# Rotary embedding on one core: tables loaded to 64 partitions and spread by a matmul, x's first piece issued by ScalarE, first group in pieces of 2, 2 and 4 rows

## The chip, the core and the metric

The kernel runs on one core of one Trainium2 chip. The metric is the device time of one execution in microseconds; the figure given for a kernel is the median of several runs. Engines are named as in the profile: PE (TensorE; PEld is its weight load), DVE (VectorE), ACT (ScalarE), POOL (GpSimd), SP (SyncE, which here only issues DMAs).

## What is computed

Rotary position embedding on x of 16 batches, 512 positions, 16 heads of 64 elements, in fp32. Each head is cut into halves of 32; cos and sin have one row of 32 per position.

```python
x = x.reshape(batch, seq, num_heads, head_dim)
x1, x2 = x[..., :half_dim], x[..., half_dim:]
rotated = np.concatenate([x1 * cos - x2 * sin, x1 * sin + x2 * cos], axis=-1)
```

x is 33.5 MB, the output as much; cos and sin are 64 KB each.

## The kernel before

The 8192 positions (batch times sequence) are cut into 8 groups of 1024. A group is 128 partitions with 8 successive positions ("rows") each: 2 batches of 64 partitions. A row is 128 x 1024 fp32, a group 4 MB, contiguous 32 KB per partition. The 64 rows are numbered u = 0 to 63, and live in a ring of 40 (RING), which is 5 groups; the result is written over x in place.

A row's result is the sum of two products. The first, t1 = x * cos, is made by DVE into PSUM (mul, L247; three buffers). The second, t2 = (halves of x swapped) * (-sin, sin), is made by POOL into SBUF (L216; six buffers), except for row 3 of each group (VROW), where DVE makes it too (L238). The sum is made in one of two ways: for rows 1, 3 and 6 of each group, PE adds t2 to t1 in PSUM by four matmuls with the identity (L187), and ACT copies the result back to x's place (L161); for the other five, DVE adds (comb, L258). DVE's order is written out: mul(u), then the add of row u - 2. A product t1 of row u needs the buffer of row u - 3, so it waits for that row's add or, where PE added, for ACT's copy.

Loads are issued by SP in order (on_sync, L138): the first group in two halves of 2 MB, the others whole. After the first half come cos and sin (L145), each to all 128 partitions (two batches need the same rows, so each row is read twice), 1 KB per partition. The first five groups' loads wait for nothing; the loads of groups 5, 6 and 7 wait until the store of group 0, 1 and 2 has landed (L141). Stores are issued by ACT between its copies (L165), one for each group, the last group in two halves.

Before the rows start, DVE copies cos into PSUM (L225) and row 3's sin with both signs (L227, L228); ACT writes sin with both signs to s_sb for POOL (L154, L155); POOL builds the identity (L198, L200); PE clears t1's banks with six matmuls of zeros (L173).

Of the kernel before, what the change touches and what calls it, by code (L numbers as in the profile page):

```python
# [6 lines left out]
def bass_split_heads_rope_kernel(  # L7
# [4 lines left out]
    num_heads: bass.AP,  # L12
    out: bass.AP,
):

# [23 lines left out]
    RING = 40  # L39
    NU = G * R  # L40

    def pieces(halved):
        return [
            (g, r, n) for g in range(G) for r, n in (((0, R // 2), (R // 2, R // 2)) if g == halved else ((0, R),))
        ]


    loads = pieces(0)
    stores = pieces(G - 1)
    load_of = [c for c, (_, _, n) in enumerate(loads) for _ in range(n)]  # L50

    def where(u):
# [9 lines left out]
    def count(flags):  # L62
        return [sum(flags[: u + 1]) for u in range(NU)]

    n_pool = count([not v for v in V2])
    n_dve = count(V2)
    n_pe = count(PE2)
    n_comb = count([not a for a in PE2])

# [6 lines left out]
    with ExitStack() as stack:  # L76
        x_sb = stack.enter_context(nc.sbuf_tensor([P, RING, H, 2, HALF], fp32))
        t2_sb = stack.enter_context(nc.sbuf_tensor([P, NT2, H, 2, HALF], fp32))
        stage = stack.enter_context(nc.sbuf_tensor([P, 2, R * HALF], fp32))
        s_sb = stack.enter_context(nc.sbuf_tensor([P, R, 2, HALF], fp32))  # L80
        ident = stack.enter_context(nc.sbuf_tensor([P, P], fp32))
        zero = stack.enter_context(nc.sbuf_tensor([P, BANK], bf16))
        tab_ps = stack.enter_context(nc.psum_tensor([P, BANK], fp32))
        t1_ps = stack.enter_context(nc.psum_tensor([P, NT1, H * HD], fp32))
        sem_in = [stack.enter_context(nc.semaphore(f"in{c}")) for c in range(len(loads))]
        sem_out = [stack.enter_context(nc.semaphore(f"out{c}")) for c in range(G - RING // R)]
# [6 lines left out]
        sem_i = stack.enter_context(nc.semaphore("ident"))  # L93
        sem_w = stack.enter_context(nc.semaphore("bits"))
        sem_p = stack.enter_context(nc.semaphore("pool"))
        sem_d = stack.enter_context(nc.semaphore("dve2"))
        sem_m = stack.enter_context(nc.semaphore("mul"))
        sem_v = stack.enter_context(nc.semaphore("comb"))
        sem_e = stack.enter_context(nc.semaphore("pe"))
        sem_a = stack.enter_context(nc.semaphore("act"))  # L100

        c_ps = tab_ps[:, 0:R * HALF].rearrange("p (r d) -> p r d", d=HALF)
        s_ps = tab_ps[:, R * HALF:R * HALF + HD].rearrange("p (t d) -> p t d", d=HALF)

        xv = x.rearrange("(g b) (s r) d -> g s b (r d)", b=BL, r=R)
        ov = out.rearrange("(g b) (s r) h d -> g s b (r h d)", b=BL, r=R)
# [22 lines left out]
        def wait_t2_free(eng, u):  # L129

            if u >= NT2:
# [3 lines left out]
                else:  # L135
                    eng.wait_ge(sem_v, n_comb[v])

        def on_sync(sp):  # L138
            for c, (g, r, n) in enumerate(loads):
                if g * R >= RING:  # L140
                    sp.wait_ge(sem_out[g - RING // R], 16)  # L141
                sp.dma_start(tile(g, r, n), part(xv, g, r, n)).then_inc(sem_in[c], 16)  # L142
                if c == 0:
                    for i, (table, sem) in enumerate(((cos, sem_cos), (sin, sem_sin))):
                        sp.dma_start(  # L145
                            stage[:, i, :],
                            table.rearrange("(s r) d -> s (r d)", r=R)[:, None, :].broadcast_to([SB, BL, R * HALF]),
                        ).then_inc(sem, 16)
            sp.wait_ge(sem_rest, 16 * (len(stores) - len(sem_out)))

        def on_scalar(ae):
            ae.wait_ge(sem_sin, 16)
            sv = stage[:, 1, :].rearrange("s (r d) -> s r d", d=HALF)
            ae.activation(s_sb[:, :, 0, :], sv, COPY, scale=-1.0)  # L154
            ae.activation(s_sb[:, :, 1, :], sv, COPY).then_inc(sem_s, 1)  # L155
            ends = {g * R + r + n - 1: (c, g, r, n) for c, (g, r, n) in enumerate(stores)}
            for u in range(NU):
                k = where(u)[2]
                if PE2[u]:
                    ae.wait_ge(sem_e, n_pe[u])  # L160
                    ae.activation(xs[:, k, :], t1_ps[:, u % NT1, :], COPY).then_inc(sem_a, 1)  # L161
                if u in ends:
                    c, g, r, n = ends[u]
                    wait_added(ae, u)
                    ae.dma_start(part(ov, g, r, n), tile(g, r, n)).then_inc(  # L165
                        sem_out[c] if c < len(sem_out) else sem_rest, 16
                    )

        def on_tensor(pe):
            pe.wait_ge(sem_z, 1)  # L170
            for k in range(NT1):
                for b in range(EH):
                    pe.matmul(  # L173
                        t1_ps[:, k, b * BANK:(b + 1) * BANK], zero[:, 0:P], zero[:], start=True, stop=True
                    ).then_inc(sem_w, 1)
            pe.wait_ge(sem_i, 2)
            for u in range(NU):
                if not PE2[u]:
                    continue
                pe.wait_ge(sem_m, u + 1)  # L180
                if V2[u]:
                    pe.wait_ge(sem_d, n_dve[u])
                else:
                    pe.wait_ge(sem_p, n_pool[u])
                t2 = t2_sb[:, u % NT2, :, :, :].rearrange("p h t d -> p (h t d)")
                for b in range(EH):
                    ins = pe.matmul(  # L187
                        t1_ps[:, u % NT1, b * BANK:(b + 1) * BANK],
                        ident[:],
                        t2[:, b * BANK:(b + 1) * BANK],  # L190
                        start=False,
                        stop=True,
                        skip_group_check=True,
                    )
                ins.then_inc(sem_e, 1)

        def on_gpsimd(pl):
            pl.memset(ident[:], 1.0).then_inc(sem_i, 1)  # L198
            pl.wait_ge(sem_i, 1)
            pl.affine_select(  # L200
                out=ident[:],
                in_=ident[:],
                compare_op=mybir.AluOpType.is_equal,
                fill=0.0,
                base=0,
                pattern=[[-1, P]],
                channel_multiplier=1,
            ).then_inc(sem_i, 1)
            pl.wait_ge(sem_s, 1)
            for u in range(NU):  # L210
                if V2[u]:
                    continue
                c, r, k = where(u)
                pl.wait_ge(sem_in[c], 16)
                wait_t2_free(pl, u)
                pl.tensor_tensor(  # L216
                    t2_sb[:, u % NT2, :, :, :], swapped(k), over_heads(s_sb[:, r]), mult
                ).then_inc(sem_p, 1)

        def on_vector(ve):  # L220
            ve.memset(zero[:], 0.0).then_inc(sem_z, 1)  # L221
            cv = stage[:, 0, :].rearrange("s (r d) -> s r d", d=HALF)
            sv = stage[:, 1, VROW * HALF:(VROW + 1) * HALF]
            ve.wait_ge(sem_cos, 16)
            ve.tensor_copy(c_ps, cv)  # L225
            ve.wait_ge(sem_sin, 16)
            ve.tensor_scalar_mul(s_ps[:, 0, :], sv, -1.0)  # L227
            ve.tensor_copy(s_ps[:, 1, :], sv).then_inc(sem_c, 1)  # L228
            ve.wait_ge(sem_c, 1)
            ve.wait_ge(sem_w, NT1 * EH)  # L230

            def mul(u):
                c, r, k = where(u)
                if u == 0 or load_of[u] != load_of[u - 1]:
                    ve.wait_ge(sem_in[c], 16)
                if V2[u]:
                    wait_t2_free(ve, u)
                    ve.tensor_tensor(  # L238
                        t2_sb[:, u % NT2, :, :, :], swapped(k), over_heads(s_ps), mult
                    ).then_inc(sem_d, 1)  # L240
# [68 lines left out]
```

## Time and profile before

| what | value |
|---|---|
| median of 7 runs | 162.04 us (162.02 to 162.95) |
| profiled execution: its own time | 162.43 us |
| profiled execution: span of its instructions | 161.0 us |
| DVE / POOL busy | 131.6 / 130.6 us |
| first row product on DVE / on POOL starts | 9.76 / 10.25 us |
| cos / sin issued | 1.46 / 2.11 us |
| first store issued (ACT's queue) | 32.08 us |
| last load issued, and lands | 96.9 and 128.8 us |
| last store issued, and its time to landing | 154.24 and 6.7 us |

The span begins with the first instruction and ends with the last; the execution's own time has 1.43 us around it. In the page, section 2 cuts the span into 40 slices of 4 us and shows each engine's busy share in tenths, the DMA engines' mean share and the GB/s that they moved. Other views give the busy times in chosen stretches, the instructions in order of time, and each DMA's issue with its time to landing. A share of the DMA engines a little above 1 in a stretch comes from packets that overlap or that began before it.

### The profile page before, as it was taken

To read this page: it belongs to the slowest core of one execution; us is meant where nothing else is said; L and a number is where in the kernel's file an instruction comes from. 1 tells how busy PE (TensorE), PEld (TensorE's weight loads), DVE (VectorE), ACT (ScalarE), POOL (GpSimd) and SP (SyncE) were. 2 spreads that over 40 slices of the span, in tenths; PEclk is the share of its full clock that TensorE was granted. 3 is DMA by queue.
4 is the path that set the end of the run, shared out by engine and by line. 5 is a ranking of instruction groups with operands and counts; after the bars stand their busy time and mean duration, and the time that the engine had idled before them with its cause. 6 is when DMAs were issued, how large, how long until landed. Compare 5 with 4: busy or idle time off the path is not lost.

```text
span 161.0 us, 579 instructions
## 1 busy us (share of the span) xinstructions
PE 85.6 (53%) x102; PEld 26.9 (17%) x102; DVE 131.6 (82%) x116; ACT 26.6 (17%) x27; POOL 130.6 (81%) x62
## 2 busy tenths in 40 slices
PE   6002928368438549439448448646426844855800
PEld 1001402112202202202202211211111210220200
DVE  0079199999699969998799989997999969996920
ACT  3010220220220220220220221022202022022020
POOL 1049999999999999999997999799979799892000
PEclk9999985555955555855555855595975595555595
DMA  4999999998999999999999999999999999999987
GB/s 138 400 446 497 407 415 480 407 391 383 407 464 431 399 464 433 399 472 431 391 474 440 391 472 440 391 464 448 391 448 456 399 440 464 399 440 448 387 370 326
DMA packets 2882, 67.39 MB, mean 419 GB/s; under 512 B 320, under 2 KB 576, under 8 KB 576
## 3 DMA queue, kind: packets, MB, share of 16 engines
q1 hardware_dynamic: 1584, 33.82, 49.8%
q10 hardware_dynamic: 1296, 33.56, 48.4%
q14 instruction: 2, 0.02, 0.0%
HBM read 33.82 MB, written 33.55 MB: 418 GB/s over the span
## 4 chain that ended last, share of the span: by engine, by line
DVE 30%; PE 23%; issue 17%; POOL 14%; ACT 6%; DMA 5%; SPq 1%; DVEq 0%; POOLq 0%
PE t_ps L187 23%; DVE x_sb L258 15%; POOL t_sb L216 14%; DVE t_ps L247 11%; ACT x_sb L161 6%; DMA stage<-in_sin_dram 5%; DVE t_sb L238 4%; SPq L142 0%; SPq L145 0%; ACT s_sb L154 0%; ACT s_sb L155 0%; DVEq L246 0%; POOLq L134 0%
## 5 line engine op out<-in xcount | busy, mean ns | idle before, releaser
L216 POOL TENSOR_TENSOR t_sb<-x_sb,s_sb 128x1024 f32<-128x1024 f32 x56 | 129.9, 2357 | 14.5 <-ACT s_sb L155 8.9
L187 PE MATMUL t_ps<-t_sb,ident 128*128 128x512 f32 x96 | 82.8, 1016 | 66.3 <-DVE t_ps L247 52.6
L247 DVE TENSOR_TENSOR t_ps<-x_sb,tab_ps 128x1024 f32<-128x1024 f32 x64 | 77.3, 1227 | 13.7 <-ACT x_sb L161 11.9
L258 DVE TENSOR_TENSOR x_sb<-t_ps,t_sb 128x1024 f32<-128x1024 f32 x40 | 48.6, 1216 | 0.0
L187 PEld LDWEIGHTS t_ps<-t_sb,ident 128*128 128x128 f32 x96 | 26.1, 299 | 122.5 <-DVE t_ps L247 87.5
L161 ACT ACTIVATE x_sb<-t_ps 128x1024 f32<-128x1024 f32 x24 | 24.6, 1024 | 119.5 <-PE t_ps L187 119.5
L238 DVE TENSOR_TENSOR t_sb<-x_sb,tab_ps 128x1024 f32<-128x1024 f32 x8 | 9.7, 1209 | 0.0
L225 DVE COPY tab_ps<-stage 128x256 f32<-128x256 f32 x1 | 0.4, 428 | 7.9 <-DMA stage<-in_cos_dram 7.9
L173 PE MATMUL t_ps<-zero 128*128 128x512 bf16 x6 | 2.7, 630 | 1.3 <-DVE zero L221 1.3
L154 ACT ACTIVATE s_sb<-stage 128x256 f32<-128x256 f32 x1 | 0.4, 416 | 7.4 <-DMA stage<-in_sin_dram 7.4
L154 ACT ACT_TABLE_LOAD x1 | 1.3, 1283 | 0.8 <-PEq L291 0.8
L173 PEld LDWEIGHTS t_ps<-zero 128*128 128x128 bf16 x6 | 0.7, 138 | 2.3 <-DVE zero L221 1.2
L221 DVE MEMSET zero<- 128x256 uint32 x1 | 0.3, 272 | 0.9 <-PEq L291 0.9
L198 POOL MEMSET ident<- 128x128 f32 x1 | 0.2, 205 | 0.3 <-POOLq L291 0.3
L155 ACT ACTIVATE s_sb<-stage 128x256 f32<-128x256 f32 x1 | 0.4, 400 | 0.0
L200 POOL TENSOR_SCALAR_AFFINE_SELECT ident<-ident 128x128 f32<-128x128 f32 x1 | 0.3, 293 | 0.1
L291 POOL MEMSET const-float32-0.0<- 128x1 f32 x1 | 0.1, 99 | 0.3 <-issue 0.3
L227 DVE TENSOR_SCALAR tab_ps<-stage 128x32 f32<-128x32 f32 x1 | 0.2, 195 | 0.0
L228 DVE COPY tab_ps<-stage 128x32 f32<-128x32 f32 x1 | 0.2, 184 | 0.0
L291 POOL MEMSET const-uint8-127<- 128x1 uint8 x1 | 0.1, 103 | 0.0
L291 POOL MEMSET const-bfloat16-1.0<- 128x1 bf16 x1 | 0.1, 102 | 0.0
L291 POOL MEMSET const-float32-1.0<- 128x1 f32 x1 | 0.1, 100 | 0.0
## 6 DMA issues: line engine op xcount, KB each, us to landing
x_sb<-in_x_dram SPq DMA_DIRECT2D x7, 4096.0 KB, 31.9
out_dram<-x_sb ACTq DMA_DIRECT2D x7, 4096.0 KB, 27.6
x_sb<-in_x_dram SPq DMA_DIRECT2D x2, 2048.0 KB, 9.8
out_dram<-x_sb ACTq DMA_DIRECT2D x2, 2048.0 KB, 7.3
stage<-in_cos_dram SPq DMA_DIRECT2D x1, 128.0 KB, 7.6
stage<-in_sin_dram SPq DMA_DIRECT2D x1, 128.0 KB, 7.3
```

Source lines behind the costliest of these rows:

```text
L154: ae.activation(s_sb[:, :, 0, :], sv, COPY, scale=-1.0)
L155: ae.activation(s_sb[:, :, 1, :], sv, COPY).then_inc(sem_s, 1)
L161: ae.activation(xs[:, k, :], t1_ps[:, u % NT1, :], COPY).then_inc(sem_a, 1)
L173: pe.matmul(t1_ps[:, k, b * BANK:(b + 1) * BANK], zero[:, 0:P], zero[:], start=True, stop=True).then_inc(sem_w, 1)
L187: ins = pe.matmul(t1_ps[:, u % NT1, b * BANK:(b + 1) * BANK], ident[:], t2[:, b * BANK:(b + 1) * BANK], start=False, stop=True, skip_group ...
L200: pl.affine_select(out=ident[:], in_=ident[:], compare_op=mybir.AluOpType.is_equal, fill=0.0, base=0, pattern=[[-1, P]], channel_multiplier=1,
L216: pl.tensor_tensor(t2_sb[:, u % NT2, :, :, :], swapped(k), over_heads(s_sb[:, r]), mult).then_inc(sem_p, 1)
L225: ve.tensor_copy(c_ps, cv)
L238: ve.tensor_tensor(t2_sb[:, u % NT2, :, :, :], swapped(k), over_heads(s_ps), mult).then_inc(sem_d, 1)
L247: ve.tensor_tensor(t1_ps[:, u % NT1, :].rearrange("p (h d) -> p h d", d=HALF), x_sb[:, k, :, :, :].rearrange("p h t d -> p (h t) d"), c_ps ...
L258: ve.tensor_tensor(xs[:, k, :], t1_ps[:, u % NT1, :], t2_sb[:, u % NT2, :, :, :].rearrange("p h t d -> p (h t d)"), add,).then_inc(sem_v, 1)
L291: nc = _bacc.Bacc("TRN2", target_bir_lowering=False, num_devices=1)
```

## The change

The tables are loaded once, to 64 partitions (stage and the new pick have 64), and one matmul with a 64 x 128 selection matrix puts partition s's rows on partitions 2s and 2s + 1, into one PSUM bank that holds cos and sin. DVE reads cos straight from there; ACT makes s_sb from there; row 3's signed sin has a bank of its own (v_ps) and is written by DVE after ACT is done. The selection matrix is built by POOL ahead of the identity. SP issues the tables first and then the loads from the second piece on; the first piece is issued by ACT as its first instruction. The first group's load is in pieces of 2, 2 and 4 rows. PE no longer waits for DVE's second product of row 3 by a semaphore of its own; DVE's later mul of the same row stands for it.

```diff
-    loads = pieces(0)
-    stores = pieces(G - 1)
+    loads = pieces(0, (2, 2, 4))
+    stores = pieces(G - 1, (4, 4))
...
-        stage = stack.enter_context(nc.sbuf_tensor([P, 2, R * HALF], fp32))
+        stage = stack.enter_context(nc.sbuf_tensor([SB, 2, R * HALF], fp32))
+        pick = stack.enter_context(nc.sbuf_tensor([SB, SB, BL], fp32))
...
-        tab_ps = stack.enter_context(nc.psum_tensor([P, BANK], fp32))
+        tab_ps = stack.enter_context(nc.psum_tensor([P, 2, R, HALF], fp32))
+        v_ps = stack.enter_context(nc.psum_tensor([P, BANK], fp32))
...
-        c_ps = tab_ps[:, 0:R * HALF].rearrange("p (r d) -> p r d", d=HALF)
-        s_ps = tab_ps[:, R * HALF:R * HALF + HD].rearrange("p (t d) -> p t d", d=HALF)
+        c_ps = tab_ps[:, 0]
+        s_ps = v_ps[:, 0:HD].rearrange("p (t d) -> p t d", d=HALF)
...
+        def load(eng, c):
+            g, r, n = loads[c]
+            if g * R >= RING:
+                eng.wait_ge(sem_out[g - RING // R], 16)
+            eng.dma_start(tile(g, r, n), part(xv, g, r, n)).then_inc(sem_in[c], 16)
+
         def on_sync(sp):
-            for c, (g, r, n) in enumerate(loads):
-                if g * R >= RING:
-                    sp.wait_ge(sem_out[g - RING // R], 16)
-                sp.dma_start(tile(g, r, n), part(xv, g, r, n)).then_inc(sem_in[c], 16)
-                if c == 0:
-                    for i, (table, sem) in enumerate(((cos, sem_cos), (sin, sem_sin))):
-                        sp.dma_start(
-                            stage[:, i, :],
-                            table.rearrange("(s r) d -> s (r d)", r=R)[:, None, :].broadcast_to([SB, BL, R * HALF]),
-                        ).then_inc(sem, 16)
+            for i, (table, sem) in enumerate(((cos, sem_cos), (sin, sem_sin))):
+                sp.dma_start(stage[:, i, :], table.rearrange("(s r) d -> s (r d)", r=R)).then_inc(sem, 16)
+            for c in range(1, len(loads)):
+                load(sp, c)
...
         def on_scalar(ae):
-            ae.wait_ge(sem_sin, 16)
-            sv = stage[:, 1, :].rearrange("s (r d) -> s r d", d=HALF)
-            ae.activation(s_sb[:, :, 0, :], sv, COPY, scale=-1.0)
-            ae.activation(s_sb[:, :, 1, :], sv, COPY).then_inc(sem_s, 1)
+            load(ae, 0)
+            ae.wait_ge(sem_t, 1)
+            ae.activation(s_sb[:, :, 0, :], tab_ps[:, 1], COPY, scale=-1.0)
+            ae.activation(s_sb[:, :, 1, :], tab_ps[:, 1], COPY).then_inc(sem_s, 1)
...
+            pe.wait_ge(sem_g, 2)
+            pe.wait_ge(sem_cos, 16)
+            pe.wait_ge(sem_sin, 16)
+            pe.matmul(
+                tab_ps[:].rearrange("p c r d -> p (c r d)"),
+                pick[:].rearrange("q s b -> q (s b)"),
+                stage[:].rearrange("q c f -> q (c f)"),
+                start=True,
+                stop=True,
+            ).then_inc(sem_t, 1)
             pe.wait_ge(sem_i, 2)
...
                 pe.wait_ge(sem_m, u + 1)
-                if V2[u]:
-                    pe.wait_ge(sem_d, n_dve[u])
-                else:
+
+                if not V2[u]:
                     pe.wait_ge(sem_p, n_pool[u])
...
         def on_gpsimd(pl):
+
+            pl.memset(pick[:], 1.0).then_inc(sem_g, 1)
+            pl.wait_ge(sem_g, 1)
+            pl.affine_select(
+                out=pick[:],
+                in_=pick[:],
+                compare_op=mybir.AluOpType.is_equal,
+                fill=0.0,
+                base=0,
+                pattern=[[-1, SB], [0, BL]],
+                channel_multiplier=1,
+            ).then_inc(sem_g, 1)
...
             ve.memset(zero[:], 0.0).then_inc(sem_z, 1)
-            cv = stage[:, 0, :].rearrange("s (r d) -> s r d", d=HALF)
-            sv = stage[:, 1, VROW * HALF:(VROW + 1) * HALF]
-            ve.wait_ge(sem_cos, 16)
-            ve.tensor_copy(c_ps, cv)
-            ve.wait_ge(sem_sin, 16)
-            ve.tensor_scalar_mul(s_ps[:, 0, :], sv, -1.0)
+            ve.wait_ge(sem_s, 1)
+            sv = tab_ps[:, 1, VROW, :]
+            ve.tensor_scalar_mul(s_ps[:, 0, :], sv, -1.0).then_inc(sem_c, 1)
             ve.tensor_copy(s_ps[:, 1, :], sv).then_inc(sem_c, 1)
-            ve.wait_ge(sem_c, 1)
+            ve.wait_ge(sem_c, 2)
             ve.wait_ge(sem_w, NT1 * EH)
```

More of the change, by code (lines that the diff above doesn't have):

```diff
@@ L40, in bass_split_heads_rope_kernel, with pieces @@
     NU = G * R
[L42 to L45, printed above, removed]
-    loads = pieces(0)
-    stores = pieces(G - 1)
+    def pieces(special, sizes):
+        return [(g, sum(ns[:i]), n) for g in range(G) for ns in ((sizes if g == special else (R,)),) for i, n in enumerate(ns)]
+    loads = pieces(0, (2, 2, 4))
+    stores = pieces(G - 1, (4, 4))
     load_of = [c for c, (_, _, n) in enumerate(loads) for _ in range(n)]
@@ L65, in bass_split_heads_rope_kernel @@
     n_pool = count([not v for v in V2])
-    n_dve = count(V2)
     n_pe = count(PE2)
@@ L95, in bass_split_heads_rope_kernel @@
         sem_p = stack.enter_context(nc.semaphore("pool"))
-        sem_d = stack.enter_context(nc.semaphore("dve2"))
         sem_m = stack.enter_context(nc.semaphore("mul"))
@@ L99, in bass_split_heads_rope_kernel @@
         sem_e = stack.enter_context(nc.semaphore("pe"))
+        sem_g = stack.enter_context(nc.semaphore("pick"))
+        sem_t = stack.enter_context(nc.semaphore("spread"))
         sem_a = stack.enter_context(nc.semaphore("act"))
-        c_ps = tab_ps[:, 0:R * HALF].rearrange("p (r d) -> p r d", d=HALF)
-        s_ps = tab_ps[:, R * HALF:R * HALF + HD].rearrange("p (t d) -> p t d", d=HALF)
+        c_ps = tab_ps[:, 0]
+        s_ps = v_ps[:, 0:HD].rearrange("p (t d) -> p t d", d=HALF)
         xv = x.rearrange("(g b) (s r) d -> g s b (r d)", b=BL, r=R)
@@ L237, in mul @@
                     wait_t2_free(ve, u)
-                    ve.tensor_tensor(
-                        t2_sb[:, u % NT2, :, :, :], swapped(k), over_heads(s_ps), mult
-                    ).then_inc(sem_d, 1)
+                    ve.tensor_tensor(t2_sb[:, u % NT2, :, :, :], swapped(k), over_heads(s_ps), mult)
                 if u >= NT1:
```

## The prediction

> **What bounds the kernel now.** I read the slices first, then the rates in chosen stretches, then who waits for DMA, then the two DMA queues' issues with their landings. In the page, the rows to compare are DMA and DVE:
>
> ```profile
> DVE  0079199999699969998799989997999969996920
> POOL 1049999999999999999997999799979799892000
> DMA  4999999998999999999999999999999999999987
> ```
>
> ```profile
> PE 85.6 (53%) x102; PEld 26.9 (17%) x102; DVE 131.6 (82%) x116; ACT 26.6 (17%) x27; POOL 130.6 (81%) x62
> ...
> q1 hardware_dynamic: 1584, 33.82, 49.8%
> q10 hardware_dynamic: 1296, 33.56, 48.4%
> ```
>
> The compute engines idle for some 10 us at the start and 7 us at the end; the DMA engines do not idle at all between. The loads' queue (q1) and the stores' queue (q10) together took 98.2% of 16 engines' span. The stretches (columns: stretch, length, busy of PE, PEld, DVE, ACT, POOL, then granted clock, DMA share, GB/s) say it more sharply:
>
> ```profile
> 2.00:33.00 31.00, 13.59 (x19) 4.84 (x18) 20.27 (x20) 3.88 (x6) 22.75 (x10) 0.84 1.02 427
> 33.00:37.00 4.00, 2.26 (x4) 0.64 (x3) 4.00 (x5) 1.02 (x1) 4.00 (x3) 0.50 0.89 295
> 37.00:128.80 91.80, 54.41 (x64) 16.76 (x63) 84.80 (x73) 15.36 (x15) 86.85 (x38) 0.61 1.01 434
> ```
>
> ```profile
> 128.80:154.00 25.20, 14.58 (x17) 4.35 (x16) 22.18 (x20) 4.91 (x5) 16.30 (x7) 0.59 1.00 430
> 154.00:156.00 2.00, 0.00 (x0) 0.00 (x0) 0.07 (x1) 0.21 (x1) 0.00 (x0) 1.00 0.60 254
> 156.00:161.00 5.00, 0.00 (x0) 0.00 (x0) 0.00 (x0) 0.00 (x0) 0.00 (x0) 0.53 0.87 367
> ```
>
> From 2 us to 154 us DMA is full: loads alone at first, loads and stores from 37, stores alone from 128.8. There is one dent at 33 to 37, where the first store joins, and one hole: 154 to 156, share 0.60. The packet records show the hole as about 0.6 us per DMA engine: the last packets of the next-to-last store end at about 155.0 and the first of the last store start at about 155.5. That store is issued at 154.24 (ACT's timeline), because the last row's add ends then. So the compute chain that the page's chain of waits follows for the whole span decides only this 0.6 us; the rest is bytes. **The kernel is DMA-bound with a small hole at its end.**
>
> The packet records give the floor: a 32 KB packet takes 1.213 us, a 16 KB one 0.611, a 1 KB table row 0.046. One of 16 engines moves 112 + 32 + 16 of them: 135.9 + 19.6 + 0.7 = 156.2 us. The first packet starts at 2.2 us, so nothing could end before 158.4. The span of 161.0 holds 2.6 us more: 0.4 idle in 2 to 3 us, 0.6 of slow first packets (mean 0.650 instead of 0.611, times 16), about 1 at the first store, 0.6 in the hole, 0.4 after the last packet; overlaps of neighbouring packets give some 0.4 back.
>
> **The change, part by part.**
>
> *Tables and x at the start.* SP's first two issues become the tables (0.80 and 1.46 us, 0.60 each); ScalarE issues x's first 1 MB at 0.80, where it now loads its function table (1.28 us; this then ends near 2.7, and nothing needs ScalarE before 4.5, so it is covered by 1.8 us). The second x piece goes from SP at 2.11 instead of 2.76, the third at 2.76. Every later load keeps its place within 0.7 us behind a queue that is 10 to 60 us deep. SP waits for nothing new. First packets follow an issue by 1.4 us (0.80 to 2.20), so DMA starts at 2.2 as before; ScalarE's first piece is 2.4 us of work, SP's second has packets from 3.5: no gap.
> *Table landing.* Today sin is issued at 2.11 and lands at 9.43, behind 2 MB of x. After: at best 1.46 + 1.4 + a few rows + 0.35 (last packet to landing) = 3.4; at worst behind the whole first megabyte, 7.0. I take 4.5, near the lower end, since the tables are ahead in their own queue.
> *Selection matmul (64x128x512 fp32).* Not in the trace; the fp32 matmul of L187 with 512 columns takes 0.59 (warm) to 1.22 us (the first at 15 us), weight load 0.29. I take 1.2, the cold end. It waits behind L173, done at 4.0, and delays nothing on PE until 15 us. Then two ACTIVATEs from PSUM, 0.40 to 0.42 as from SBUF (up to 1.02 by L161, which has four times the elements): s_sb is ready at about 6.5. The 0.43 us copy of cos goes; the two 0.2 us ones on DVE now follow ScalarE: DVE starts at about 6.8. POOL's second memset and select (0.5 us, as L198 and L200) delay ident from 1.4 to 1.9; it is needed at 15.
> *x's first piece.* 1 MB lands between 5.7 (alone) and 7.0 (sharing with the second piece from 3.5). So **POOL starts at about 6.8 instead of 10.25: 3.4 us earlier**, between 2.5 and 4.3. The second piece has landed by 8.8 (needed at 11.4), the third by 13.6 (needed by POOL at 13.7: three rows of 2.31 on): level.
> *PE's dropped wait on DVE's second product* is the same order by the program: mul follows it on DVE; zero.
>
> *What becomes of 3.4 us.* Loads 2 to 5 (groups 1 to 4) land at 24.0, 33.8, 51.2, 70.6, the next at 90.1, 109.4, 128.8: 9.7 us apart alone, 19.4 beside stores, i.e. half the rate each. A first store 3.4 us earlier costs the loads half the rate 3.4 us longer: the last load lands 3.4 later, less twice the saved 0.3 us below: at 131.9. So loads come later while rows are wanted earlier. POOL today has one wait for x (0.9 us); after, with 16.2 us per group from 6.8: group 1 wanted 23.0 (lands 23.7), group 4 at 72.4 (73.6), groups 5 to 7 each some 3 us early. The gain of the start is eaten by **POOL waits on x of some 6 to 11 us**, the last for the last load.
> Does the last store still come earlier? DVE runs some 7 us behind POOL (mul of group 7 starts at 135.1, POOL at 128.84), so it rides over most of this: 154.24 - 3.4 = 150.8. The lower bound from the last load: POOL 131.9 + 7 x 2.31 = 148.1, add and issue 149.5. The upper: a refill like the first group's, POOL's start to store 32.08 - 10.25 = 21.8, less the two products of the next group (2.3) = 19.5: 151.4. To close the hole it must be issued by 153.3. So the hole closes: **-0.6 us**, between 0 and -0.8.
> *Bytes.* 64 partitions instead of 128: 8 table rows per engine fewer, 8 x 0.046 = -0.37. 16 packets of 8 KB instead of 8 of 16 KB: by the line through 1, 16 and 32 KB one takes 0.310, so +0.07 (if smaller first packets were as slow as today's first, +0.6). **-0.3 us.**
> The start may move either way: two queues instead of one could fill the 0.4 idle and 0.6 slow packets, or lengthen them: 0, from -0.7 to +0.6.
>
> Sum: 161.0 - 0.6 - 0.3 = 160.1 us of span. The profiled execution took 162.43 with that span; the median of the seven is 162.04. Taken from the median: **161.1 us**.
>
> [...] The traced rows come first: the half-group stores of 2 MB with 16 KB packets move at 0.611 us a packet, the rate of 4 MB. [...]
>
> **Rivals.**
> *Compute decides, the 3.4 us pass through:* 158.6. For it: the chain of waits lies on DVE and PE to the last store. Against: it would end below the packets' floor of 158.4 - 0.3 by span 157.6. Chance 0.03.
> *The hole stays:* the last rows, late by the last load, end at 154 again; only bytes are saved: 161.7. For it: DVE has short waits on ACT and PE that a dry POOL lengthens, as in the first group (3.3 us). Needs 2.5 us more than my upper bound. 0.16.
> *The start comes late:* ScalarE's issue falls behind its function table (today at 0.80, 1.28 long), or its queue starts slower: the last store's first packet came 1.2 us after its issue, but the first store's 4.9, beside loads. With tables only 0.2 us of work, DMA then idles to 3.5: +1.3 - 0.9: 162.4. 0.10, of it 0.04 past the bound.
> *Starved loads, slower:* the place is the last load. If stores get more than half of the engines, or start still earlier, it lands so late that 19.5 us of rows behind it pass 154.24 + 0.9 + 0.5: from a landing at 136.1 on, 7.3 us later than today. At 138 the store is issued at 157.5, the span is 164.2, the time about 165. Against: both queues show half each. 0.06.
> *The forecast*, 160.4 to 161.5: 0.65.
>
> **Numbers.** About 0.3% (0.5 us) is what a measurement of this kernel can tell from no change. Faster by more: 0.65 + 0.03 = 0.68, and 0.01 of the hole's case = 0.69. Same: 0.15 + 0.06 = 0.21. Slower: 0.04 + 0.06 = 0.10. The range from 160.4 (start gains 0.7) to 162.4 (late start) leaves out 0.03 + 0.06 and some edges.
>
> **What would show it.** First mul at 6 to 7.5 us, first store issued at 28 to 29.5, last load landing at 131 to 133, POOL waits on x of 6 us or more; last store issued before 153.3; no slice pair at 0.60 before the end; POOL's and DVE's busy unchanged. Wrong would be: a DMA start after 2.7, a last load at 129 or earlier with compute ending 3 us earlier, or a share under 0.95 anywhere between 5 and 155.

## The result, and the profile after

The changed kernel took 163.51 us in the median of 13 runs, the kernel before 162.42 us on the same chip: a ratio of 1.0059, 95% interval 1.0043 to 1.0075. It is slower by about 0.95 us, where 0.9 us less had been forecast. In kernels of this study whose rows start at 11.5 us or later, some executions (five of twelve in three of the four) took 164.2 to 166.2 us; they, and single outliers of others, are left out of the comparisons.

Each run also gives the span of the instructions, so the time splits in two. The kernel before has 1.42 us around its span (1.37 to 1.47 in 23 runs of one job); the changed kernel has 2.1 in the median. That is about 0.65 of the 0.95 us. The span itself went from 161.0 (162.42 - 1.42) to 161.2, which is most of the rest; medians need not add up exactly. The profiled execution of the changed kernel has a span of 162.3, 1.1 above its median, so its tail is read here for its form, not for its size.

The start first. These are rows of the page's section 6 (issue, engine, count, KB, us to landing) after the change:

```profile
x_sb<-in_x_dram ACTq DMA_DIRECT2D x1, 1024.0 KB, 6.0
x_sb<-in_x_dram SPq DMA_DIRECT2D x1, 1024.0 KB, 7.4
stage<-in_cos_dram SPq DMA_DIRECT2D x1, 64.0 KB, 2.3
stage<-in_sin_dram SPq DMA_DIRECT2D x1, 64.0 KB, 5.7
```

cos, issued at 0.81, takes 2.3 us; sin, of the same size and issued 0.6 us later, takes 5.7 and lands at 7.1. The timeline shows what followed (start, length, engine and line):

```profile
7.25 1.65 PE L180 MATMUL tab_ps<-stage,pick 64*128 64x512 f32 x2 [3.25 <-DMA stage<-in_sin_dram]
8.94 0.38 ACT L155 ACTIVATE s_sb<-tab_ps 128x256 f32<-128x256 f32 x1 [6.19 <-PE tab_ps L180]
9.22 0.38 ACT L156 ACTIVATE s_sb<-tab_ps 128x256 f32<-128x256 f32 x1
9.63 0.20 DVE L246 TENSOR_SCALAR v_ps<-tab_ps 128x32 f32<-128x32 f32 x1 [8.44 <-ACT s_sb L156]
```

The matmul is two passes on PE, 1.65 us and not 1.2. POOL starts at 9.68, 0.6 us earlier than before instead of 3.4; DVE's first product comes at 9.96, 0.2 later (6 to 7.5 was forecast).

The rows nevertheless ended early. The first store is issued at 31.23 (28 to 29.5 was forecast), the last at 151.13 instead of 154.24. This row is the last store's issue, with its time to landing; before, it was 6.7:

```profile
out_dram<-x_sb ACTq DMA_DIRECT2D x1, 2048.0 KB, 11.1
```

The stretches at the end (columns as in the prediction):

```profile
131.90:151.10 19.20, 9.01 (x13) 2.53 (x12) 18.59 (x17) 4.10 (x4) 16.21 (x7) 0.68 0.99 426
151.10:156.00 4.90, 0.00 (x0) 0.00 (x0) 0.00 (x0) 0.00 (x0) 0.00 (x0) 0.50 0.98 418
156.00:160.00 4.00, 0.00 (x0) 0.00 (x0) 0.00 (x0) 0.00 (x0) 0.00 (x0) 0.50 0.96 410
160.00:162.30 2.30, 0.00 (x0) 0.00 (x0) 0.00 (x0) 0.00 (x0) 0.00 (x0) 0.50 0.14 57
```

The hole of 154 to 156 is gone (share 0.98), as forecast. In its place the last 2.3 us have a share of 0.14: most DMA engines are done while a few still write. The store's 16 parts land between 159.83 and 162.23; before, between 160.73 and 160.97 (these are the trace's landing records). The median part comes 0.25 us earlier than before (160.55 against 160.81), the last 1.26 later, and the last one counts.

Last, an instruction transfer (queue 8) that the kernel before doesn't have, in the stretch from 162 to 166 us, after the end of the span:

```profile
DMA packets 1, 0.02 MB, mean 4 GB/s; under 512 B 0, under 2 KB 0, under 8 KB 0
## 3 DMA queue, kind: packets, MB, share of 16 engines
q8 instruction: 1, 0.02, 1.5%
```

It is one packet of 16,384 B, from 163.6 to 164.5 us.

### The profile page after: what moved, and what is told of

The parts are those of the page before. It is cut to its first block, busy times and chain, and to the rows that moved or that the text cites. A ratio compares the mean times of both kernels' runs of the same rounds, so it can differ in the third digit from the quotient of the medians.

```text
span 162.3 us, 578 instructions
## 1 busy us (share of the span) xinstructions
PE 82.8 (51%) x104; PEld 25.3 (16%) x104; DVE 131.0 (81%) x115; ACT 26.5 (16%) x27; POOL 131.2 (81%) x64
## 4 chain that ended last, share of the span: by engine, by line
DVE 34%; PE 23%; issue 14%; POOL 12%; ACT 5%; DMA 4%; SPq 0%; DVEq 0%; POOLq 0%
PE t_ps L197 22%; DVE x_sb L275 16%; DVE t_ps L264 14%; POOL t_sb L238 12%; ACT x_sb L162 4%; DVE t_sb L257 4%; DMA stage<-in_sin_dram 4%; PE tab_ps L180 1%; SPq L147 0%; ACT s_sb L155 0%; ACT s_sb L156 0%; DVEq L263 0%; POOLq L135 0%; DVEq L274 0%; DVEq L261 0%
## 5 line engine op out<-in xcount | busy, mean ns | idle before, releaser
L197 PE MATMUL t_ps<-t_sb,ident 128*128 128x512 f32 x96 | 78.4, 966 | 61.8 <-DVE t_ps L264 44.8
L197 PEld LDWEIGHTS t_ps<-t_sb,ident 128*128 128x128 f32 x96 | 24.2, 277 | 115.9 <-DVE t_ps L264 82.2
L257 DVE TENSOR_TENSOR t_sb<-x_sb,v_ps 128x1024 f32<-128x1024 f32 x8 | 9.7, 1210 | 0.0
L180 PE MATMUL tab_ps<-stage,pick 64*128 64x512 f32 x2 | 1.7, 929 | 3.3 <-DMA stage<-in_sin_dram 3.3
L155 ACT ACTIVATE s_sb<-tab_ps 128x256 f32<-128x256 f32 x1 | 0.4, 384 | 6.2 <-PE tab_ps L180 6.2
L211 POOL TENSOR_SCALAR_AFFINE_SELECT pick<-pick 64x128 f32<-64x128 f32 x1 | 0.7, 698 | 0.1
L156 ACT ACTIVATE s_sb<-tab_ps 128x256 f32<-128x256 f32 x1 | 0.4, 378 | 0.0
```

What stands on the lines that cost most here:

```text
L155: ae.activation(s_sb[:, :, 0, :], tab_ps[:, 1], COPY, scale=-1.0)
L156: ae.activation(s_sb[:, :, 1, :], tab_ps[:, 1], COPY).then_inc(sem_s, 1)
L180: pe.matmul(tab_ps[:].rearrange("p c r d -> p (c r d)"), pick[:].rearrange("q s b -> q (s b)"), stage[:].rearrange("q c f -> q (c f)"), st ...
L197: ins = pe.matmul(t1_ps[:, u % NT1, b * BANK:(b + 1) * BANK], ident[:], t2[:, b * BANK:(b + 1) * BANK], start=False, stop=True, skip_group ...
L211: pl.affine_select(out=pick[:], in_=pick[:], compare_op=mybir.AluOpType.is_equal, fill=0.0, base=0, pattern=[[-1, SB], [0, BL]], channel_m ...
L257: ve.tensor_tensor(t2_sb[:, u % NT2, :, :, :], swapped(k), over_heads(s_ps), mult)
```

## The experiments

### One part of the change at a time

**First piece by SP** (the changed kernel):

```diff
-            for c in range(1, len(loads)):
+            for c in range(len(loads)):
                 load(sp, c)
...
-            load(ae, 0)
```

> The changed kernel with x's first piece issued by SP, third in its queue behind both tables; ScalarE issues no load. Theory A (every DMA engine is busy from 2 us on, and the one that lags most ends the span, so an earlier start of the rows buys nothing): sin lands near 3.5 us instead of 7.1, POOL starts near 6.8 instead of 9.7, the last store is issued near 150 us, and the span stays at 160.5 to 161.5; if ScalarE's early load also made the 0.6 us by which the time outside the span grew (1.43 us before, 1.92 after), the time is 162.0 to 162.6, else 162.6 to 163.3. Rival B (the late sin is what kept the gain away): the span falls by the 3 us that POOL starts earlier, to 158 to 159, the time to 160 to 161.

Ratio 1.0116 (1.0081 to 1.0151): span 161.7, outside 2.06. The tables land 2.1 and 2.2 us after their issue, POOL starts at 7.69. Starting two microseconds earlier than the changed kernel bought nothing; rival B is out. In the profiled execution the last store was issued only at 153.07, where theory A had about 150. The span grew, and the first stretch gives a likely reason:

```profile
2.00:4.00 2.00, 2.00 (x6) 0.54 (x4) 0.00 (x0) 0.08 (x1) 0.29 (x1) 1.00 0.60 139
```

x's first piece is SP's third issue, and DMA has only the tables until then: 139 GB/s, where the kernel before had 279 in this stretch and the changed kernel 242. The 280 KB that are missing against the kernel before are 0.65 us at 430 GB/s, the 206 KB against the changed kernel 0.48. The 2 us outside are there without ScalarE's load, so that isn't their cause.

**First half by ScalarE** (the kernel before, tables first on SP):

```diff
+            ae.dma_start(tile(*loads[0]), part(xv, *loads[0])).then_inc(sem_in[0], 16)
             ae.wait_ge(sem_sin, 16)
...
             for c, (g, r, n) in enumerate(loads):
+                if c == 0:
+                    continue
```

> The kernel before with one part of the change: ScalarE issues x's first half (2 MB), SP issues the tables first, still to 128 partitions. If an engine finishes one queue's whole transfer before it turns to the other, sin waits behind all of x's half and lands near 9 us as before, cos near 3; rows start at 9.5 to 10, and the span stays within 0.3 us of 161.0. If queues alternate packet by packet, sin lands near 4.5 and POOL starts near 5.5 to 8.5. If the longer time outside the span comes with ScalarE's early load, it is about 2.0 us here, the time 162.8 to 163.3; else 1.4 us and a time of 162.2 to 162.6.

Ratio 1.0007 (0.9989 to 1.0025), span 160.75, outside 1.40: no cost, no gain. The landings bear on the question of the queues:

```profile
x_sb<-in_x_dram ACTq DMA_DIRECT2D x1, 2048.0 KB, 8.3
x_sb<-in_x_dram SPq DMA_DIRECT2D x1, 2048.0 KB, 12.0
stage<-in_cos_dram SPq DMA_DIRECT2D x1, 128.0 KB, 3.2
stage<-in_sin_dram SPq DMA_DIRECT2D x1, 128.0 KB, 7.8
```

sin takes 7.8 us behind 2 MB of the other queue and took 5.7 behind 1 MB. In the changed kernel sin's first packet starts at 5.38, when the first engine is through its eight packets of x. In this kernel sin lands at 9.3 (issued at 1.46), near the 9 of the first reading set down for this run and not the 4.5 of the second. But the first doesn't hold whole: sin's packets begin at 5.91, while no engine is through x's piece before 7.98, though no part of sin is complete before 8.15. How an engine divides its time between two queues isn't shown.

**Tables on 64 partitions and matmul** (the changed kernel with x's first half by SP, ahead of the tables):

```diff
-    loads = pieces(0, (2, 2, 4))
+    loads = pieces(0, (4, 4))
...
+            load(sp, 0)
             for i, (table, sem) in enumerate(((cos, sem_cos), (sin, sem_sin))):
...
-            load(ae, 0)
```

> The kernel before in order and pieces (x's first half, then the tables, all by SP, pieces of 4 and 4), with the change's tables on 64 partitions, selection matrix and matmul. The tables land as before near 9.0, then 1.7 us of matmul, so rows start near 11.5 instead of 9.8 to 10.3. Theory A: the span stays at 160.6 to 161.6, as the start isn't what the end waits for, if the last store still is issued by 155.5. Rival B: the start's 1.5 us are seen in full, a span of 162.5. If the longer time outside the span comes from the instructions of this part (two more on POOL, one matmul on PE), it is about 2.0 us here.

Ratio 1.0028 (1.0000 to 1.0056): span 160.3 against 160.7, outside 1.97. A span shorter by 0.4 us would be the size of the saved bytes (0.37 in the working), although rows start at 12.4. But it is the median of seven executions that lie between 160.1 and 161.9, and the padded variant below, with the same loads, doesn't repeat it; so the gain isn't shown. What this part clearly brings is the time outside.

**Pieces of 2, 2 and 4** (the kernel before):

```diff
-    loads = pieces(0)
+    loads = [(0, 0, 2), (0, 2, 2), (0, 4, 4)] + pieces(0)[2:]
```

> The kernel before with the first group in pieces of 2, 2 and 4 rows, nothing else: x's first megabyte by SP, then the tables, then the rest. Tables land near 6.7 instead of 9.4, POOL starts near 7.5 instead of 10.25. Theory A: last store issued near 151.5, span unchanged within 0.5 us of 161.0, since no DMA engine has idle time to give. Rival B: the span falls by 2.7 us to about 158.3. If the longer time outside the span came with this part (one more load), it is about 2.0 us here.

Ratio 1.0026 (1.0012 to 1.0040): span 161.2 against 160.7, outside 1.42. POOL starts at 7.9, the last store is issued at 152.05, and the span is longer. POOL's waits show where the early start went (total, times, longest):

```profile
POOL t_sb L216 <- DMA x_sb<-in_x_dram: 11.4, 5, 3.2
```

11.4 us of waits for x instead of 0.9: that step of the prediction holds. In 2 to 4 us DMA moves 221 GB/s instead of 279, and from 2 to 13 us 383 instead of 398: by then 0.4 us of bytes behind.

**Pieces of 4, 2 and 2** (the kernel before):

```diff
-    loads = pieces(0)
+    loads = [(0, 0, 4), (0, 4, 2), (0, 6, 2)] + pieces(0)[2:]
```

> The kernel before with the first group in pieces of 4, 2 and 2 rows: as many loads as with 2, 2 and 4, but the first packets are of 16 KB as before and the tables land as before near 9.3. If the pieces' part lengthened the span by 0.5 us (161.2 against 160.7) because of small first packets or the earlier rows, the span is 160.6 to 160.9 here; if 8 KB packets or one more load cost it wherever they stand, 161.1 to 161.3.

Ratio 1.0010 (0.9982 to 1.0037), span 160.8, the same as before in that job. So neither 8 KB packets nor the one load more cost anything by themselves here. Small pieces at the very start, or the earlier rows that they bring, did (+0.5 us of span); which of the two isn't separated.

**The changed kernel with halves of 4 and 4:**

```diff
-    loads = pieces(0, (2, 2, 4))
+    loads = pieces(0, (4, 4))
```

> The changed kernel with the first group in halves of 4 and 4 rows as before: tables on 64 partitions with the matmul, first half by ScalarE. If the pieces lengthen the span by 0.5 us as they did alone, it falls from 161.2 to 160.3 to 160.7 here, with the 2.0 us outside a time of 162.3 to 162.7. If the rest of the change does it, the span stays near 161.2 and the time near 163.2.

Ratio 1.0009 (0.9990 to 1.0027), span 160.8 (before 161.1 in this job), outside 2.07. Without the small pieces the span is no longer above that of before; the 0.65 us outside remain.

### Does the last store's issue decide?

**Last store later** (the changed kernel):

```diff
                     c, g, r, n = ends[u]
+                    if u == NU - 1:
+                        for i in range(4):
+                            if i:
+                                ae.wait_ge(sem_idle, i)
+                            ae.activation(idle[:], s_sb[:].rearrange("p r t d -> p (r t d)"), COPY).then_inc(sem_idle, 1)
```

> The changed kernel with four more copies on ScalarE (128x512, into a scratch tile) ahead of the last store's issue, so that it comes about 2.5 us later, near 153.5 instead of 151.1. Theory A (after the change the last store is early by more than the DMA engines can use, and the slowest of them ends the span): the span stays at the changed kernel's 160.4 to 162.3, median near 161.2, and the landings of the last store lie closer together. Rival (the issue of the last store decides): 2.5 us more, 163 to 164 of span, 165 to 166 of time.

Ratio 1.0106 (1.0071 to 1.0141), but span 161.7 in the median against 161.2: half a microsecond for copies that were to hold the store back by 2.5. That lies in theory A's range; the rival's 163 to 164 is out. In the profiled execution the rows came late as well, so the store was issued at 155.66, and there it does decide:

```profile
out_dram<-x_sb ACTq DMA_DIRECT2D x1, 2048.0 KB, 6.7
```

155.66 + 6.7 is its span of 162.4. The profiled executions line up. In the eight whose last store is issued at 153.73 (tables' part) or later, among them the kernel before (154.24) and this one, the last part lands 6.6 to 6.8 us after the issue. In the twelve where it is issued at 150.7 to 153.1, the span is 160.3 to 162.8 without any order by issue. There another number fits: the last store's last part lands 4.81 to 4.85 us after the next-to-last store's last part, and the last store's 16 parts are spread almost as widely as those of the store before it (2.40 and 2.41 us in the changed kernel, 0.89 and 0.90 with the first half by ScalarE). Eight packets of 0.61 us are 4.9 us, so the engine that lags writes its share of the last store with no pause. In these profiles the end passes from the slowest DMA engine to the issue between 153.1 and 153.7. The rows' end moves by 3 us between executions even with the same start (150.91 in the run below, where the rows start as in the kernel before), and the span doesn't follow.

**First store later** (the kernel before):

```diff
-            ends = {g * R + r + n - 1: (c, g, r, n) for c, (g, r, n) in enumerate(stores)}
+            ends = {g * R + r + n - 1 + (3 if g == 0 else 0): (c, g, r, n) for c, (g, r, n) in enumerate(stores)}
```

> The kernel before with the first group's store issued three rows later (about 38 instead of 32 us); the rest as it is. Theory C (each us by which loads and stores run side by side costs the engines a little, so an earlier start lengthens the span): the last load lands some 6 us earlier, near 123, and the span falls by 0.3 to 1.0 us, to 160.0 to 160.7, as in the kernel with the tables' part alone, whose rows started 2 us later and whose span was 160.4. Rival: the order of loads and stores doesn't matter, the span stays at 160.8 to 161.2. A loss (161.5 and more) would say that the stores' backlog runs dry near the end.

Ratio 1.0060 (1.0045 to 1.0075), span 161.8: theory C falls, and so does its rival. The last load lands at 128.78, as before, not near 123. The reading set down for a loss doesn't fit either: the last store is issued at 150.91, so the stores didn't run dry near the end. Stretches of this kernel:

```profile
40.00:44.00 4.00, 2.14 (x3) 0.92 (x4) 3.40 (x4) 0.54 (x1) 4.00 (x3) 0.81 0.99 328
44.00:64.00 20.00, 10.82 (x14) 3.03 (x12) 18.28 (x17) 3.73 (x4) 20.00 (x10) 0.61 1.00 433
64.00:76.00 12.00, 5.24 (x8) 1.60 (x8) 11.93 (x11) 2.42 (x3) 12.00 (x6) 0.86 1.00 421
76.00:79.00 3.00, 2.79 (x4) 0.97 (x4) 2.97 (x4) 0.00 (x0) 3.00 (x2) 0.60 1.03 328
```

There are two dents instead of one, at 328 GB/s. The loads of groups 1 to 4 are done at 64.8, and the next one is issued only when the late first store has landed, at 64.25; its first packet starts at 68.2, so the loads' queue was empty for some 4 us, in which the stores alone kept DMA full. The second dip comes 8 us after the loads are back, just ahead of the first packets of the third group's store (77.99), as the first dip comes just ahead of those of the first store (43.85). Why DMA dips there isn't shown. (433 - 328) x 3 us is 0.3 MB, 0.7 us, and 421 instead of 433 over the 12 us before it is another 0.3: about the 1.1 us of span that are lost. The loss follows the stretch with an empty loads' queue; that this stretch causes it is likely, not shown.

### The time outside the span

It comes with the tables' part. Single executions escape it: one of the changed kernel has 1.39 us outside, one with halves of 4 and 4 has 1.46. Two kernels split that part by engine, each the kernel before with idle instructions.

```diff
+            pl.memset(pick[:], 1.0).then_inc(sem_g, 1)
+            pl.wait_ge(sem_g, 1)
+            pl.affine_select(out=pick[:], in_=pick[:], ...).then_inc(sem_g, 1)
             pl.memset(ident[:], 1.0).then_inc(sem_i, 1)
```

> The kernel before plus the change's two GpSimd instructions that build the selection matrix; nothing uses it. The question is which instructions of the tables' part bring the 0.55 us outside the span, which came with a 16 KB instruction transfer after the last instruction in the three kernels that have this part and in none of the three that lack it. If GpSimd's instructions cross a block of code, the transfer is there, the time outside the span is 1.9 to 2.0 us and the time 162.6 to 162.9. If it is PE's, nothing changes: 1.4 us outside, 162.0 to 162.4.

```diff
             pe.wait_ge(sem_i, 2)
+            pe.wait_ge(sem_cos, 16)
+            pe.wait_ge(sem_sin, 16)
+            pe.matmul(v_ps[:], ident[0:SB, :], stage[0:SB].rearrange("q c f -> q (c f)"), start=True, stop=True)
```

> The kernel before plus one fp32 matmul of 64x128x512 on PE (rows of the identity by the staged tables) into a spare bank, which nothing reads. If PE's instructions cross a block of code, the 16 KB instruction transfer is there, 1.9 to 2.0 us lie outside the span and the time is 162.6 to 162.9; if it is GpSimd's, 1.4 us and 162.0 to 162.4. Both at 1.4 would mean another engine, or the sum of both.

GpSimd's: ratio 1.0007 (0.9996 to 1.0018), outside 1.40, no transfer. PE's: 1.0052 (1.0037 to 1.0068), span 160.9, outside 1.99, transfer after the end. One matmul that nothing reads, finished before the first row needs PE, makes the kernel half a per cent slower. This kernel also repeats the reading of the tail: its last store was issued at 151.32, three microseconds earlier than in the kernel before, took 9.4 to land, and the span is 160.8.

What about the matmul does it? Four more kernels vary it:

```diff
# 128 rows
+            pe.matmul(v_ps[:], ident[:], stage[:].rearrange("q c f -> q (c f)"), start=True, stop=True)
# 64 rows, bf16, no wait
+            pe.matmul(v_ps[:], zero[0:SB, 0:P], zero[0:SB, :], start=True, stop=True)
# the waits alone
+            pe.wait_ge(sem_cos, 16)
+            pe.wait_ge(sem_sin, 16)
# fp32, 128 rows and 128 columns, no wait
+            pe.matmul(v_ps[:, 0:P], ident[:], ident[:], start=True, stop=True)
```

> The kernel before plus the same idle fp32 matmul as in the run with PE's one more matmul, but over all 128 partitions (128x128x512) instead of 64; the number of PE's instructions is the same in both. Theory D (a matmul over 64 rows, not the length of the code, brings the 16 KB instruction transfer after the end): no such transfer, 1.4 us outside the span, 162.0 to 162.4. Rival (one more PE instruction brings it): the transfer is there, 1.9 to 2.2 us outside, 162.6 to 163.2.

> The kernel before plus one idle bf16 matmul over 64 rows (zeros, 64x128x512), right behind the six that clear the banks; fewer instructions than the fp32 one. Theory D says that the transfer after the end and 1.9 to 2.2 us outside the span are there, 162.6 to 163.2, and that fp32 has nothing to do with it. If only the fp32 matmul of the tables does it, 1.4 us and 162.0 to 162.4.

> The kernel before; PE only waits for the semaphores of the cos and sin loads ahead of its first sum, which by then have long come; no matmul is added. If a wait of PE on a DMA's semaphore is what brings the transfer after the end, it is there: 1.9 to 2.2 us outside the span, 162.6 to 163.2. If the fp32 matmul brings it, 1.4 us and 162.0 to 162.4.

> The kernel before plus one fp32 matmul of the identity by itself (128x128x128) that starts a spare bank, without any wait for a DMA. If an fp32 matmul that starts a bank brings the transfer after the end, it is there: 1.9 to 2.2 us outside, 162.6 to 163.2. If the wait on a DMA's semaphore brings it, 1.4 us and 162.0 to 162.4.

128 rows: 1.0041 (1.0023 to 1.0058), outside 2.01, transfer. bf16: 0.9996 (0.9977 to 1.0014), 1.42, none. Waits alone: 0.9992 (0.9979 to 1.0006), 1.43, none. fp32 without waits: 0.9987 (0.9973 to 1.0001), 1.43, none. Theory D is out, and no single property remains. The tables' part with the selection padded to 128 rows says the same:

```diff
-        stage = stack.enter_context(nc.sbuf_tensor([SB, 2, R * HALF], fp32))
-        pick = stack.enter_context(nc.sbuf_tensor([SB, SB, BL], fp32))
+        stage = stack.enter_context(nc.sbuf_tensor([P, 2, R * HALF], fp32))
+        pick = stack.enter_context(nc.sbuf_tensor([P, SB, BL], fp32))
...
             ve.memset(zero[:], 0.0).then_inc(sem_z, 1)
+            ve.memset(stage[SB:P], 0.0).then_inc(sem_z, 1)
```

> The tables' part alone (as in the run of that part), with selection matrix and staged tables padded by zeros to 128 partitions, so that the selection matmul is over 128 rows; the loads still go to 64 partitions. Theory D: no transfer after the end, 1.4 us outside; the span as in that run, 160.1 to 160.4, so 161.5 to 161.9, 0.2 to 0.4% faster than before. If the tables' part brings the transfer in another way, 2.0 us outside and 162.1 to 162.4.

1.0048 (1.0020 to 1.0077), outside 2.01, transfer there. Its span is 161.1 against 160.8 before, where 160.1 to 160.4 was expected: a miss of its own.

So three kernels only moved PE's code by waits:

```diff
             pe.wait_ge(sem_i, 2)
+            for _ in range(5):
+                pe.wait_ge(sem_z, 1)
+                pe.wait_ge(sem_i, 2)
```

(6 instead of 5 in the kernel before.)

> The changed kernel with five more waits on PE (on semaphores that have long come), so that PE's code has 234 instructions instead of 229, as long as in kernels without the transfer. Theory E (only the length of PE's code, by where it falls in blocks, decides): no transfer after the end, 1.4 us outside instead of 2.1, the span as in the changed kernel near 161.2: 162.5 to 162.8. Rival (something in the tables' part brings it whatever the length): 2.0 us outside, 163.2 to 163.6.

> The kernel before with six more waits on PE and no matmul: 238 instructions instead of 232. Theory E: the transfer is there, 1.9 to 2.2 us outside the span, 162.6 to 163.3, though nothing but waits that cost nothing was added. Rival (a combination in the added matmul): none, 1.4 us, 162.0 to 162.5.

> The tables' part alone with the same five waits on PE, 234 instructions. Theory E: no transfer, 1.4 us outside, the span as in the tables' part, 160.1 to 160.4 where the rows keep ahead of the DMA engines: 161.5 to 161.9, 0.2 to 0.4% faster than before. As the rows start 2 us later here, executions in which they end after the DMA engines' other work may be at 163 or more. Rival: 2.0 us outside, 162.1 to 162.4.

Both theories missed. The transfer is in all three, as theory E had it for one of them only, but it has moved into the span: at 150.1, 148.4 and 146.9 us. This is the changed kernel with five waits, in the stretch from 149 to 152:

```profile
q10 hardware_dynamic: 59, 1.05, 82.3%
q8 instruction: 1, 0.02, 2.0%
```

The time outside falls to 1.25, 1.24 and 1.21 us, below that of the kernel before, and the span grows: 161.9 (changed, 161.2 without the waits), 161.3 (before, 160.9), 161.8 (tables' part, 160.3). Ratios 1.0050 (1.0025 to 1.0074), 1.0017 (1.0005 to 1.0029) and 1.0043 (1.0026 to 1.0059). The second is the clean one: waits that cost nothing in themselves bring the transfer into the kernel before. So in these kernels PE's code decides whether the transfer comes and when; by which property isn't shown. The blocks of code that theory E and two of the expectations speak of were the author's assumption: what the traces show is one packet of 16,384 B. It takes 0.9 us of a DMA engine while the last stores are written (q10 has 82.3% of the 16 engines in the stretch above); that the span grows by 0.4 to 0.7 us (1.5 in the tables' part, of which few executions could be compared) fits an end set by the slowest engine. How a transfer after the end lengthens the execution isn't shown: in the changed kernel's profile the packet ends 2.3 us after the span, while 1.9 us in all lie outside it. About 0.6 us more outside the span is what came with it here (2.0 instead of 1.42).

What places it is open. PE's code, counted in the compiled program, is 232 to 236 instructions in kernels without the transfer, 229, 230, 237 with it after the end, 234 and 238 with it inside, so its length alone doesn't decide. Within each family the order is by length, though: among the variants of the kernel before, none up to 236, after the end at 237, inside at 238; among those with the tables' part, after the end at 229 and 230, inside at 234.

## Why the prediction was wrong

**The bound was right, its last consequence wrong.** DMA is full from 2 us on (a mean share of 0.98 or more in each of five stretches between 2 and 156 us in the changed kernel), and rows that start earlier only wait for x (POOL 8.7 us in the changed kernel, 11.4 with the pieces alone; 6 to 11 forecast). The last load lands at 131.9 as forecast, and the last store is issued at 151.13 (150.8 forecast). That these numbers agree is partly luck: they were worked out from rows that start 3.4 us earlier, and the rows started 0.6 earlier; the first store came 0.85 us earlier, the last load 3.2 us later. The last store's issue varies by 3 us between executions with the same start, and with rows from 7.69 us (first piece by SP) it came at 153.07.

**The step that failed is "So the hole closes: -0.6 us".** The hole closed and nothing was gained. The 0.6 us were a mean over 16 engines, and the slowest of them had none of it. In the kernel before, the next-to-last store's last part landed at 156.13, and the last store's first packets had started at 155.5; 156.13 + 4.84 us, the time that the lagging engine needs for the next store in the twelve profiles above, is 160.97, which is when the last part did land. So in the profiled execution the worth of the hole was nothing. The hole let the fast engines wait for the slow ones. Once the stores follow each other without it, the lag stays to the end, a spread of 2.4 us instead of 0.24. The floor should have been drawn for the slowest engine. Where the engines lie closer together the hole does cost: in the kernel with the idle matmul over 128 rows the next-to-last store's last part landed at 155.75, the last store was issued at 154.57, and its last part came at 161.19, 0.6 later than 155.75 + 4.84. What sets the spread is open.

**"Taken from the median" assumed that what lies around the span stays 1.43 us.** It became 2.1, and with it came an instruction transfer after the end that follows PE's code. No step of the prediction looked at the code. This is two thirds of the loss.

**Bytes, -0.3 us:** not shown. The tables' part alone had 0.4 us less span, its padded variant 0.3 more. The pieces cost +0.5 alone. The bracket held "+0.6 if smaller first packets were as slow as today's first"; the value taken was +0.07. Behind other transfers (pieces of 4, 2 and 2) the smaller packets cost nothing (160.8 both), and whether packets or earlier rows make the 0.5 isn't separated.

**The start, 3.4 us earlier:** 0.6. Two sizes were off. One is sin's landing at 4.5: it was 7.1, the bracket's upper end, since its packets started only when an engine was through its piece of x (5.38). The other is the matmul at 1.2 (1.65): L187 has 96 records on PE for 48 matmuls of the code, two for each of the three rows of a group that PE adds, so 1.22 was the price of one pass of two. The 0.59 us that is called warm there was measured at 20.05 us, at a granted clock of 1.00; at 0.50 a pass mostly took 1.06. That warmth is the cause isn't shown. Neither mattered to the time, as the run with SP's early tables shows.

**ScalarE's issue** came at 0.80 ahead of its function table (1.28 us from 1.47), so the rival of a late start didn't occur; nor did starved loads. The rival "the hole stays" came nearest on the span (161.0 - 0.3 by its sum, 161.2 found), for a wrong reason. None of the slower cases was the one that came.

No kernel of the study was faster than the one before. The tables' part has its shorter span only with rows that start at 12.4 us, and loses it outside the span.

## What to carry to other kernels

Here all DMA engines were busy nearly from end to end (a mean share of 0.98 or more in five stretches between 2 and 156 us in the changed kernel), so what was left to gain lay in the bytes and at the start and end of DMA itself, and the slowest engine's finish was the end: read the spread of the last landings (2.40 us, 0.24 in the kernel before), not the mean share, before a late gap is counted as time to win. Compare the span and what lies around it separately: waits that cost nothing in themselves brought a 16 KB instruction transfer into the span (161.3 instead of 160.9), and a matmul that nothing reads brought it behind the end (1.99 us outside instead of 1.42). Two queues were not shared finely here: cos, issued with the other queue's 1 MB, took 2.3 us; sin, issued 0.6 us later, 5.7. So a small table load that must come early is best issued no later than the other queue's large piece.

## What the runs showed of the hardware

- A 16,384 B instruction transfer that follows PE's code took 0.9 us. With it after the end, about 0.6 us more lay outside the span (2.0 instead of 1.42); with it among the last stores the span was 0.4 to 0.7 us longer, and 1.21 to 1.25 lay outside.
- A 64 KB load behind another queue's 1 MB took 5.7 us, without it 2.2.
- Just ahead of the first store's first packets DMA fell to 295 (kernel before) or 328 GB/s for 4 us; in the kernel whose loads' queue ran empty from 64 to 68 us it fell once more, to 328 for 3 us.
- Where the last store was issued early, its 16 parts were spread as widely as those of the store before (0.8 to 2.5 us), and its last part landed 4.81 to 4.85 us after that store's last; issued at 153.7 us or later, they lay within 0.1 to 0.3 us.
- An fp32 matmul of 64x128x512 shows as two passes of 0.80 and 1.06 us, 1.65 together as they overlap.
- The rows' last store varied from 150.9 to 154.6 us with the same start, while the span stayed within 160.5 to 161.7.
